# The last store as a plain DMA of the framework, with ScalarE taking the waits for the six stores ahead of it

## Chip, cores, metric

One core of one Trainium2 chip. The metric is the device time of one execution in microseconds (us), as the median of several runs. The "span" of a profile is the time from the core's first to its last instruction, some 1.8 us shorter than the device time here (123.5 against 125.36 us in the profiled run of the kernel before).

## The reference

Sixteen products of 512 x 512 matrices in float32, the second operand transposed:

```python
def setup_inputs():
    batch, m, k, n = 16, 512, 512, 512
    # a: (batch, m, k), b: (batch, n, k), standard normal float32
def reference(a, b):
    return np.matmul(a, b.transpose(0, 2, 1)).astype(np.float32)
```

## The kernel before

Loads, casts, transposes, products, evictions and stores run on their own engines and talk through semaphores that the kernel allocates itself. All of it stands in one hand-written section (`tile_critical`) inside which the framework adds no waits. When a section is left, the framework closes it: the engine that leads the section (SyncE, if nothing else is said) raises a semaphore, waits for the engines, and only then goes on. In the trace a closing shows as a branch, an event, a drain and a no-op: instructions without data, which here only wait for semaphores or count them up (records of 33, 17, 7 and 13 ns in the kernel before). A second, tiny section holds one wait, that for the last store.

```python
    STORES = "SSSSOSOSOSSOOOOOO"          # GpSimd stores outputs 0 to 7
    LATE = {11: (8, 9), 13: (10, 11), 15: (12, 13)}   # SyncE stores 8 to 15
    NO = 7                                 # output buffers
    ...
        def store(n):
            engine = nc.gpsimd if n < STORES.count("S") else nc.sync
            engine.wait_ge(s_out, n + 1)   # ScalarE counts finished outputs
            engine.dma_start(
                out[n].rearrange("(p j) n -> p j n", j=J), ob[:, n % NO]
            ).then_inc(landed(n)[0], 16)
        ... # loads, with late stores between them
        store(batch - 2)
        store(batch - 1)
        for n in range(batch - NO, batch - 1):
            nc.sync.wait_ge(*landed(n))    # stores 9 to 14 have landed
        ... # programs of GpSimd, VectorE, ScalarE, TensorE

    with tc.tile_critical(no_gpsimd_drain=True):
        nc.sync.wait_ge(*landed(batch - 1))   # store 15 has landed
```

## Time and profile before

| | before |
|---|---|
| device time, median | 125.48 us (125.31 to 125.68, 6 runs) |
| span of the profiled run | 123.5 us |
| mean rate from HBM and to it | 407 GB/s |
| ScalarE's last copy ends | 113.474 us |
| last store issued / landed | 113.499 / 122.217 us |
| SyncE joins the barrier at the end | 122.698 us |
| last instruction ends | 123.549 us |

The first three rows are from the results and the page. The others, with three decimals, are records of the trace: starts of single instructions, and the times at which a DMA adds to its semaphore. The trace has 16 such additions for each store; a store has landed when the last has come. I read each as one of the core's 16 DMA engines having done its part; the trace itself doesn't name the engine. Read the table from below: between the last landing and the end of the span lie 1.332 us in which no byte moves (the last packet of the trace ends at 121.751). The lines of the profile are shown in the prediction.

### The profile page before, as it was taken

The numbers are of one execution on the slowest core, as the hardware profiler recorded it, in microseconds if no ns is written. First come the engines' busy times: TensorE is split into PE (matmuls) and PEld (weight loads), VectorE is DVE, ScalarE is ACT, GpSimd is POOL, SyncE is SP. The second block draws the span as 40 slices with busy tenths as digits, with TensorE's granted clock in tenths as the row PEclk, the third lists the DMA queues.
The fourth block names the chain that finished last, engine by engine and source line by source line (L and its number), as shares of the span: only waits on it lengthen the run. The fifth ranks groups of instructions, "written<-read, shape, count | busy, mean of one in ns | idle before, by whom it ended". The sixth has DMA issues, their size and how long they took to land. (4 is left out here: it accounts for less than half of the span.)

```text
span 123.5 us, 2364 instructions
## 1 busy us (share of the span) xinstructions
PE 90.7 (73%) x768; PEld 55.8 (45%) x768; DVE 67.9 (55%) x96; ACT 68.1 (55%) x130; POOL 5.9 (5%) x14
## 2 busy tenths in 40 slices
PE   0000089999899999989998999899999946994000
PEld 0000079546734774476467447644764535441000
DVE  0000597891898389568928991894787078400000
ACT  4000063458946885595769558937876069555000
POOL 2000000000000160001010230000000000000000
PEclk9999999999999999999999999999999999999955
DMA  4999999999999999999999999999999999999990
GB/s 127 419 446 435 424 424 430 424 424 424 430 430 435 424 403 385 461 390 427 454 400 454 424 414 454 411 432 446 416 438 419 416 427 422 430 424 427 430 385 11
DMA packets 4608, 50.33 MB, mean 407 GB/s; under 512 B 512, under 2 KB 512, under 8 KB 512
## 3 DMA queue, kind: packets, MB, share of 16 engines
q1 hardware_dynamic: 3312, 39.85, 76.2%
q0 software_dynamic: 1152, 8.39, 16.1%
q10 hardware_dynamic: 144, 2.10, 4.3%
HBM read 33.55 MB, written 16.78 MB: 407 GB/s over the span
## 5 line engine op out<-in xcount | busy, mean ns | idle before, releaser
L255 PE MATMUL ps<-tb,ta 128*128 128x512 bf16 x256 | 57.8, 379 | 0.5
L213 ACT COPY ob<-ps 128x512 f32 x64 | 34.5, 588 | 28.5 <-PE ps L255 24.6
L195 ACT COPY ta<-tp 128x512 bf16<-128x512 bf16 x64 | 32.8, 610 | 15.4 <-PE tp L236 15.4
L255 PEld LDWEIGHTS ps<-tb,ta 128*128 128x128 bf16 x256 | 24.1, 97 | 30.7 <-issue 4.0
L236 PE MATMUL tp<-ident,ha 128*128 128x128 bf16 x256 | 19.6, 230 | 19.3 <-PEq L141 19.3
L236 PEld LDWEIGHTS tp<-ident,ha 128*128 128x128 bf16 x256 | 16.6, 103 | 23.1 <-issue 21.3
L176 DVE COPY tb<-tp 128x1024 bf16<-128x1024 bf16 x32 | 21.2, 684 | 4.8 <-DVEq L141 4.8
L236 PE MATMUL tp<-ident,hb 128*128 128x128 bf16 x256 | 18.1, 227 | 2.2 <-PEq L141 2.2
L236 PEld LDWEIGHTS tp<-ident,hb 128*128 128x128 bf16 x256 | 16.1, 102 | 2.6 <-issue 2.6
L160 DVE CAST ha<-ld 128x1024 bf16 x8 | 5.5, 686 | 13.7 <-DVEq L141 13.7
L171 DVE COPY ha<-wa 128x2048 bf16<-128x2048 bf16 x8 | 5.5, 692 | 13.6 <-DVEq L141 13.6
L166 DVE CAST wa<-ld 128x2048 bf16 x8 | 9.8, 1227 | 0.0
L166 DVE CAST wb<-ld 128x2048 bf16 x8 | 9.7, 1218 | 0.0
L160 DVE CAST hb<-ld 128x1024 bf16 x8 | 5.5, 688 | 6.4 <-DVEq L141 6.4
L109 POOL DMA_DIRECT2D out_dram<-ob x8 | 5.2, 655 | 65.2 <-DMA ld<-in_b_dram 41.1
L175 DVE COPY hb<-wb 128x2048 bf16<-128x2048 bf16 x8 | 5.5, 684 | 0.1
L163 DVE CAST ha<-ld 128x1024 bf16 x8 | 5.5, 686 | 0.0
L163 DVE CAST hb<-ld 128x1024 bf16 x8 | 5.5, 683 | 0.0
L186 ACT ACT_TABLE_LOAD x1 | 1.3, 1283 | 1.5 <-SPq L44 1.5
L80 POOL TENSOR_SCALAR_AFFINE_SELECT ident<-ident 128x128 bf16<-128x128 bf16 x1 | 0.3, 282 | 0.2 <-POOL ident L78 0.2
L78 POOL MEMSET ident<- 128x128 bf16 x1 | 0.2, 204 | 0.5 <-SPq L44 0.5
L186 ACT COPY one<-const-float32-1.0 128x1 f32<-128x1 f32 x1 | 0.2, 191 | 0.0
(4 smaller groups left out, 0.4 us busy)
## 6 DMA issues: line engine op xcount, KB each, us to landing
ld<-in_a_dram SPq DMA_DIRECT2D x8, 2048.0 KB, 26.3
ld<-in_b_dram SPq DMA_DIRECT2D x7, 2048.0 KB, 29.8
out_dram<-ob POOLq DMA_DIRECT2D x8, 1024.0 KB, 29.0
out_dram<-ob SPq DMA_DIRECT2D x8, 1024.0 KB, 19.6
ld<-in_b_dram ACTq DMA_DIRECT2D x1, 2048.0 KB, 12.2
```

The lines of the kernel that those rows point to most:

```text
L109: engine.dma_start(out[n].rearrange("(p j) n -> p j n", j=J), ob[:, n % NO]).then_inc(landed(n)[0], 16)
L160: nc.vector.tensor_copy(out=h[:, :J, :], in_=src[:, :J, :HK]).then_inc(s_cd, 1)
L163: nc.vector.tensor_copy(out=h[:, J:, :], in_=src[:, J:, :HK]).then_inc(s_c, 1)
L166: nc.vector.tensor_copy(out=w[:], in_=src[:, :, HK:]).then_inc(s_w, 1)
L171: nc.vector.tensor_copy(out=ha[:], in_=wa[:]).then_inc(s_ca, 1)
L175: nc.vector.tensor_copy(out=hb[:], in_=wb[:]).then_inc(s_cb, 1)
L176: nc.vector.tensor_copy(out=tb[:, ko, :], in_=tp[:, 2 + ko % 2].rearrange("k j p -> k (j p)"),).then_inc(s_eb, 1)
L186: nc.scalar.copy(out=one[:], in_=nc.const_aps.tensor(1.0, (P, 1), f32))
L195: c = nc.scalar.copy(out=ta[:, ko, e * J * P:(e + 1) * J * P].rearrange("k (j p h) -> k j p h", j=J, h=2), in_=tp[:, ko % 2, :, e * HP:(e ...
L213: c = nc.scalar.copy(out=dst[:, j, :].rearrange("m (p j) -> m p j", j=2 * J), in_=ps[:, j, :].rearrange("m (j p) -> m p j", j=2 * J),)
L236: t = nc.tensor.transpose(tp[:, 2 * x + g, j, :], h[:, j, g * P:(g + 1) * P], ident[:])
L255: t = nc.tensor.matmul(ps[:, j, :], ta[:, ko, (e * J + j) * P:(e * J + j + 1) * P], tb[:, ko, :].rearrange("k (j p) -> k j p", j=2 * J)[:, ...
```

## The change

Its intent is to let the end of the kernel wait for the last store without a section around that wait. The last store is no longer issued in the first section but behind all sections, as a DMA that the framework tracks. The framework's own end of the kernel waits for such DMAs anyway. The six waits for the stores ahead of it must then not hold SyncE up, since SyncE is to issue the last store. They go into the second section, which is now led by ScalarE, idle by then. The extra dependency only fixes the order in the program.

```diff
         store(batch - 2)
-        store(batch - 1)
-        for n in range(batch - NO, batch - 1):
-            nc.sync.wait_ge(*landed(n))
 ...
-    with tc.tile_critical(no_gpsimd_drain=True):
-        nc.sync.wait_ge(*landed(batch - 1))
+    with tc.tile_critical(sync_engine=act, no_gpsimd_drain=True):
+        for n in range(batch - NO, batch - 1):
+            nc.scalar.wait_ge(*landed(n))
+    waits = nc.cur_bb.bb.instructions[-1]
+    last = nc.sync.dma_start(
+        out[batch - 1].rearrange("(p j) n -> p j n", j=J), ob[:, (batch - 1) % NO]
+    )
+    tc.add_manual_dep(
+        last.ins,
+        waits.name,
+        mybir.DependencyInfo(mybir.DependencyClass.NoSync, mybir.DependencyReason.DATA),
+        reason="order of issue",
+    )
```

## The prediction

> **What bounds the kernel now.** I read the page first (rows of slices, DMA queues), then the waits of SyncE's queue, then single lines of SyncE in narrow windows at the end of the span, and last the records of the trace one by one to the nanosecond; times below with three decimals are from those records. The page says that the kernel is a stream of transfers:
>
> ```profile
> PE 90.7 (73%) x768; PEld 55.8 (45%) x768; DVE 67.9 (55%) x96; ACT 68.1 (55%) x130; POOL 5.9 (5%) x14
> ...
> DMA  4999999999999999999999999999999999999990
> GB/s 127 419 446 435 424 424 430 424 424 424 430 430 435 424 403 385 461 390 427 454 400 454 424 414 454 411 432 446 416 438 419 416 427 422 430 424 427 430 385 11
> ...
> q1 hardware_dynamic: 3312, 39.85, 76.2%
> q0 software_dynamic: 1152, 8.39, 16.1%
> q10 hardware_dynamic: 144, 2.10, 4.3%
> HBM read 33.55 MB, written 16.78 MB: 407 GB/s over the span
> ```
>
> The reader is to see that the DMA row is at 9 in 38 of 40 slices while the busiest compute engine has 73%: 50.3 MB at the some 425 GB/s of the middle slices are 118 us of the 123.5. Only the last slice is empty of transfers. So a change that moves no bytes can save only at the two ends. The chain of compute ends early:
>
> ```profile
> 112.38 0.36 ACT ob L213
> 112.74 0.06 issue
> 112.80 0.05 ACTq L213
> 112.85 0.04 issue
> 112.89 0.59 ACT ob L213
> ```
>
> ScalarE's last copy ends at 113.48, 10 us before the end; what remains is the drain of stores. SyncE's waits after 112 us:
>
> ```profile
> SPq L127 <- DMA out_dram<-ob: 5.8, 3, 2.4
> SPq L109 <- ACT ob L213: 1.8, 1, 1.8
> SPq L295 <- DMA out_dram<-ob: 1.7, 1, 1.7
> ```
>
> L109 is the issue of the last store, which waits for ScalarE; L127 are the waits for the six other late stores, and L295 that for the last store. Issue and landing of the last store, from the DMA view of 112 to 124 us, and then SyncE's own instructions in 122.2 to 122.5 and 122.5 to 122.65:
>
> ```profile
> out_dram<-ob SPq DMA_DIRECT2D x1, 1024.0 KB, 8.7
> ```
>
> ```profile
> L295 SPq EVENT_SEMAPHORE  x1: 1698/1698/1698, 120.5 to 120.5; - x1
> L295 SPq COMPARE_BRANCH  x1: 33/33/33, 122.3 to 122.3; - x1
> ```
>
> ```profile
> L268 SPq EVENT_SEMAPHORE  x1: 17/17/17, 122.4 to 122.4; - x1
> ```
>
> ```profile
> L268 SPq DRAIN  x1: 7/7/7, 122.5 to 122.5; - x1
> L268 SPq NOP  x1: 13/13/13, 122.6 to 122.6; - x1
> ```
>
> The wait of 1698 ns ends with the last store's landing. After it SyncE still runs the closing instructions of the second section (L268) before it may join the barrier at the end. That stretch is serial, with nothing beside it.
>
> [...] the L268 instructions last 7 to 17 ns, yet their starts, 122.432, 122.517 and 122.590, are 73 to 85 ns apart. So starts must be subtracted, not durations added. [...] this trace has a record of 33 ns but 155 ns from its start to the next start (122.277 to 122.432; 119.809 to 119.964 across two branches, too), and I use 155. [...] they land at 114.824, 117.290, 119.728 and 122.217, one per 2.45 us, that is 428 GB/s. [...] the 13 instruction-fetch packets in the trace all come before the first instruction.
>
> **The change, part by part.**
> 1. Removed: SyncE's waits at L127. They overlap the transfers of the last stores (the last of them ends at 119.77, the last landing is at 122.217). Worth 0.
> 2. Moved: the last store. Before, SyncE waits directly for ScalarE's copy count and starts the issue at 113.499, 16 ns after the count at 113.483. Now the first section must close first. SyncE tells the engines early (its last issue there is that at 111.320), ScalarE's drain comes after its copy, some 113.50; then SyncE passes a wait, a no-op and one branch to the issue. The old close of that section at 120 us gives the steps: wait for ScalarE to no-op 72 ns (120.201 to 120.273), no-op to next 73 (120.273 to 120.346), branch 155. Together 0.30, so the issue starts near 113.8, not 113.5. Is that on the path? The first issue of the kernel (ScalarE's, at 0.91) had its first packet at 1.937, 1.03 us later: descriptors of the last store would be ready near 114.85. The engines finish the store ahead of it between 117.6 and 119.25 (its 16 completion packets). Slack 2.8 us on the fastest engine. Worth 0; time from issue to landing should shrink from 8.7 to about 8.4 us.
> 3. Moved: the six waits, to ScalarE. The latest lands at 119.728. By the instruction order of the built program ScalarE then passes five more waits (64 ns each, as 120.415 to 120.479), a branch (155), an event (85), a drain (73), a no-op (44) and a branch (155): 0.83 us, so it is at the end barrier near 120.6, 1.6 us before the last landing. Worth 0.
> 4. Removed from behind the last landing: the section's branch, event, drain and no-op on SyncE. In the new order the wait for the framework's DMA count is followed by the drain that heads the end block. Before, branch start to start of that drain is 122.277 to 122.634, 0.357 us. After, that drain stands where the branch stood. Saved: 0.357, all on the path. By steps: branch 0.155 + event 0.085 + drain 0.073 + no-op 0.044 = 0.357.
> 5. Added: two semaphores (ScalarE's of the second section, the framework's DMA count), so the clearing of semaphores in the end clears 36, not 34. In the trace 34 clears stretch from 123.052 to 123.226, 5.3 ns each: +0.011 on the path.
> 6. Unchanged: bytes, queue and shape of the last store (128 rows of 2,048 floats on the same queue), all loops, the barrier and clear after SyncE's arrival (122.698 to 123.55).
>
> Sum: 0 + 0 + 0 - 0.357 + 0.011 = -0.35 us. 125.49 - 0.35 = 125.14, 0.28% less; the span should go from 123.5 to 123.2.
>
> **The rivals.**
> (a) The later issue is exposed: if the transfers needed the last store's descriptors earlier than I think, up to 0.30 would come back and the time would be about 125.45. For it: nothing[...]. Against: 2.8 us of slack[...]. It would take a stall over 2.8 us to lose anything.
> (b) ScalarE's closing chain replaces SyncE's: SyncE's final wait also asks for ScalarE's count of that section. If the chain were to come after the last landing the saving would vanish, and the time be 125.5 or more. The 1.6 us speak against it; its length would have to triple.
> (c) The framework's closing drain costs more after a DMA of its own than the 7 ns of the old one: then perhaps half of the saving remains, 125.3. In the trace every drain of SyncE has 7 ns, so I take this as unlikely.
> (d) An engine takes longer to the barrier: GpSimd has a drain of 714 ns at 120.084 in the old kernel. It now starts earlier, near 113.6, so it stays hidden.
> (e) Compute or transfers shift by other reasons. The streams are the same instruction by instruction up to 111 us, so only run-to-run noise, 125.47 to 125.68 in three runs, remains.
>
> **Range and chances.** The step sizes leave perhaps 0.08 us of doubt about the saving, and the three runs scatter by 0.2, with their median near the low side, so 125.14 with 0.25 below and 0.3 above: 124.90 to 125.45, which holds rival (c) and most of (a). A change of 2% is 2.5 us, seven times the whole stretch after the landing that the change touches; 2% slower would need a stall over 5 us. I put 0.01 on faster and 0.01 on slower.
>
> **What would show each step.** Part 2: SyncE's last issue starts near 113.8 and lands after about 8.4 us; the landing itself stays at 122.2. Part 3: ScalarE's last wait of the second section ends near 119.75, and ScalarE is in the end barrier before 121. Part 4: behind the last landing SyncE shows a wait and two drains, no event and no no-op, and GpSimd's barrier step comes 0.16 us after the landing, where it was 0.51 (122.730; 0.513 - 0.357). Part 5: the clear record is 223 ns before, some 234 after. I am wrong if the last landing itself moves by more than 0.1 us, if SyncE after the landing waits for ScalarE, or if the store's issue comes after 116 us.

The sum: -0.357 + 0.011 = -0.346 us, from parts 4 and 5. In the paragraph with most of the cuts, "they" are the last four stores. Part 2 and rival (a) speak of descriptors; the trace shows packets alone. That the last store could have its first packet near 114.85 was my estimate, from the 1.03 us between the kernel's first issue and its first packet.

## The result, and the profile after

The changed kernel takes 125.15 us (median of 6 runs, 124.99 to 125.43), the kernel before 125.48 us (6 runs). The ratio is 0.9976, with a 95% interval of 0.9961 to 0.9990. Ratios in this document are the mean time of one kernel's fast runs over that of the other's of the same rounds, so not quite the ratio of the medians; in the experiments the profiled run is left out of them. All runs were fast, that is, none was more than 1.5% above the fastest of its kernel. The gain of 0.33 us is there, but small.

SyncE's waits after 112 us in the changed kernel (us in total, times, longest):

```profile
SPq L109 <- ACT ob L210: 10.1, 1, 10.1
SPq L304 <- DMA out_dram<-ob: 7.0, 1, 7.0
SPq L44 <- PEq L44: 0.9, 1, 0.9
SPq L304 <- PEq L304: 0.7, 2, 0.6
SPq L44 <- ACTq L44: 0.7, 1, 0.7
```

The three waits of L127 for stores are gone. One wait of 7.0 us for a store is left, in the end block (L304, 1.7 us at L295 before). New are the two waits of L44, for TensorE and ScalarE: SyncE now stands at the close of the first section before its last issue. That issue, and then SyncE's instructions in 122.4 to 122.6 and all engines' of L304 in 122.6 to 122.7:

```profile
L270 SPq DMA_DIRECT2D out_dram<-ob x1: 332/332/332, 115.0 to 115.0; - x1
...
DMA to landing us min/median/max: 7.4/7.4/7.4
```

```profile
L304 SPq EVENT_SEMAPHORE  x1: 28/28/28, 122.5 to 122.5; - x1
L304 SPq DRAIN  x1: 7/7/7, 122.6 to 122.6; - x1
```

```profile
L304 SPq DRAIN  x1: 7/7/7, 122.6 to 122.6; - x1
L304 POOLq EVENT_SEMAPHORE  x1: 17/17/17, 122.7 to 122.7; - x1
```

Behind the last landing there are a wait and two drains, and GpSimd follows at once. The branch, event, drain and no-op of before (L295 and L268 in the prediction) have no counterpart. In the records, counted from the last landing: before, branch at 0.060, event 0.215, drain 0.300, no-op 0.373, drain 0.417, joining drain 0.481, end 1.332 us. After: wait 0.016, drain 0.089, joining drain 0.149, end 1.001 us. So 0.331 us less from the last landing to the end, and the medians differ by 0.33.

The record of 1698 ns in the prediction is a wait that shows inside its own record. In the kernels before and after, only event records that wait on two semaphores show this (713, 867 and 1698 ns, of 7 before and 8 after); none of the 290 and 291 that wait on one has a record over 51 ns. The wait for the last store has 1698 ns before, where its semaphore is the second of two, and 28 ns after, where it is the first.

The profiled run doesn't show that gain in its span: 123.5 us both times. Its last landing came at 122.474 us, 0.257 later than before. It was behind by 0.10 us already at 61 us, at an instruction that the change doesn't touch (SyncE's last load issue, at 61.091 against 60.985). How far the landing wanders without any change is the first thing that the experiments measure.

One more thing is later: the last issue, at 115.037. ScalarE's last copy ended 1.38 us later than before (114.853), because TensorE was slower just then. The stretch from 104 to 108 us, before and then after (columns: stretch, length, busy time and count of PE, PEld, DVE, ACT and POOL, then granted clock, the share of its full clock that TensorE had, DMA share, GB/s):

```profile
104.00:108.00 4.00, 3.88 (x36) 2.38 (x37) 1.85 (x3) 2.62 (x6) 0.00 (x0) 1.00 1.01 426
```

```profile
104.00:108.00 4.00, 3.69 (x29) 3.00 (x30) 2.20 (x4) 2.22 (x5) 0.00 (x0) 0.60 1.02 428
```

The granted clock was 0.60 there. The unchanged kernel, run again below, had 0.63 in the same stretch and its last issue at 114.797, so this is no effect of the change. The transfers (426 and 428 GB/s) didn't notice.

### The profile page after: what moved, and what is told of

Same layout as the page of the kernel before. It is cut to its first block, busy times and chain, and to the rows that moved or that the text cites. A ratio compares the mean times of both kernels' runs of the same rounds, so it can differ in the third digit from the quotient of the medians.

```text
span 123.5 us, 2365 instructions
## 1 busy us (share of the span) xinstructions
PE 91.8 (74%) x768; PEld 57.0 (46%) x768; DVE 68.1 (55%) x96; ACT 68.1 (55%) x130; POOL 6.2 (5%) x14
## 5 line engine op out<-in xcount | busy, mean ns | idle before, releaser
L233 PE MATMUL tp<-ident,ha 128*128 128x128 bf16 x256 | 20.1, 233 | 19.5 <-PEq L138 19.5
L233 PE MATMUL tp<-ident,hb 128*128 128x128 bf16 x256 | 18.8, 232 | 2.4 <-PEq L138 2.4
L233 PEld LDWEIGHTS tp<-ident,hb 128*128 128x128 bf16 x256 | 16.8, 105 | 2.8 <-issue 2.8
```

What stands on the lines that cost most here:

```text
L233: t = nc.tensor.transpose(tp[:, 2 * x + g, j, :], h[:, j, g * P:(g + 1) * P], ident[:])
```

## The experiments

Theory: what was gained is the closing of a section that SyncE went through behind the last landing; the landing itself doesn't move. Rivals: the plain DMA lands or is counted faster; or it is the move of the six waits, or the new time of issue, that gains. Nine more runs were made, all correct, each in five rounds and against the unchanged kernel on the same chip. They came on two chips, on which its median was 125.30 and 125.40 us. From each profile I took the last landing, and the time from it to SyncE's joining drain and to the end:

| kernel | median us | ratio to before (95%) | last landing | to joining drain | to end |
|---|---|---|---|---|---|
| before (first profile) | 125.48 | | 122.217 | 0.481 | 1.332 |
| before, again | 125.49 | 1.0012 (0.9997 to 1.0026) | 122.427 | 0.481 | 1.332 |
| changed (first profile) | 125.15 | 0.9976 (0.9961 to 0.9990) | 122.474 | 0.149 | 1.001 |
| changed, again | 125.12 | 0.9985 (0.9973 to 0.9998) | 122.149 | 0.150 | 1.002 |
| waits on SyncE behind the store | 125.56 | 1.0018 (1.0004 to 1.0031) | 122.270 | 0.519 | 1.380 |
| five sections | 128.37 | 1.0238 (1.0225 to 1.0252) | 122.373 | 3.486 | 4.337 |
| all waits in the second section | 125.75 | 1.0028 (1.0013 to 1.0043) | 122.213 | 0.824 | 1.675 |
| last store 3 us later | 125.14 | 0.9979 (0.9966 to 0.9991) | 122.321 | 0.144 | 0.997 |
| plain store, waits kept | 127.19 | 1.0143 (1.0128 to 1.0158) | 124.052 | 0.134 | 0.994 |

### Both kernels once more

No edit.

> The kernel before, unchanged, against itself: the size of what is no effect. Theory (closing steps behind the last landing) and every rival: ratio 1.000 within 0.001. From the last landing to SyncE's drain that joins the barrier 0.48 us, as in the first profile. If the ratio differs from 1 by 0.002 or more, the change's 0.24% can't be told from scatter.

> The changed kernel again, on the same chip as the others of this set. Theory: ratio 0.9973 (125.15 over 125.48), landing to barrier drain 0.15 us as in its first profile; the issue of the last store 0.2 us after ScalarE's last copy, and landing to the end 1.00 us against 1.33. If the first result came from a lucky set of runs: ratio 0.999 to 1.000.

The kernel before, against itself, gave 1.0012, a little more than the 0.001 that I had allowed. So ratios of this size can't be read to better than about 0.001, and the times alone would be thin evidence for 0.0024. The profiles are sharper. From the landing to the end both kernels repeat to 1 ns (1.332 and 1.332; 1.001 and 1.002), while the landing itself wanders by 0.21 us in the kernel before and by 0.33 in the changed one. All scatter lies ahead of the landing, all of the gain behind it. In this set the means of the two repeated kernels are 125.50 (6 runs) and 125.12 us (5 runs), a difference of 0.38. The issue came 0.186 us after ScalarE's last copy.

### The plain store with the six waits on SyncE behind it

```diff
-        store(batch - 1)
-        for n in range(batch - NO, batch - 1):
-            nc.sync.wait_ge(*landed(n))
 ...
+    nc.sync.dma_start(out[batch - 1]..., ob[:, (batch - 1) % NO])
     with tc.tile_critical(no_gpsimd_drain=True):
-        nc.sync.wait_ge(*landed(batch - 1))
+        for n in range(batch - NO, batch - 1):
+            nc.sync.wait_ge(*landed(n))
```

> The last store is the framework's plain DMA, as in the change, but the six waits stand in a section on SyncE behind it, so that this section waits for the plain DMA too and closes behind the last landing. Theory (the gain is the closing of a section, no longer behind the last landing): the gain is gone, ratio to before 1.000 (within 0.001), some 0.48 us from landing to the barrier drain. Rival 1 (the plain DMA itself lands or is counted faster): the gain stays, ratio 0.9975. Rival 2 (the gain comes from the later issue of the last store or from the six waits leaving the first section): the gain stays too, since both are as in the change.

The gain is gone: the ratio is 1.0018, and the rivals' 0.9975 is far outside the interval. It is even a little over the 1.000 of the theory; of that, the stretch from landing to end explains 0.05 us (1.380 against 1.332), and the rest is within what the kernel before shows against itself. SyncE's L268 instructions of this kernel (all of them), then its L296 instructions from 122.2 to 123:

```profile
L268 SPq NOP  x2: 13/13/13, 115.2 to 122.7; - x2
L268 SPq EVENT_SEMAPHORE  x1: 17/17/17, 122.5 to 122.5; - x1
L268 SPq DRAIN  x1: 7/7/7, 122.6 to 122.6; - x1
```

```profile
L296 SPq EVENT_SEMAPHORE  x2: 17/22/28, 122.3 to 122.9; - x2
L296 SPq DRAIN  x2: 7/7/7, 122.7 to 122.8; - x2
L296 SPq COMPARE_BRANCH  x1: 33/33/33, 122.4 to 122.4; - x1
```

The last store is a plain DMA and issued as in the change (114.776), but branch, event, drain and no-op stand behind its landing again, since the section behind it also waits for it. A plain DMA alone is worth nothing. What counts is that no section closes behind it.

### Five sections instead of one

```diff
+    for _ in range(5):
-    with tc.tile_critical(no_gpsimd_drain=True):
-        nc.sync.wait_ge(*landed(batch - 1))
+        with tc.tile_critical(no_gpsimd_drain=True):
+            nc.sync.wait_ge(*landed(batch - 1))
```

> The kernel before with the second section five times instead of once; four more closings behind the last landing, with no new transfer to wait for. Theory: by the starts in the profile before, one more closing is branch 155 + event 85 + drain 73 + no-op 73 + no-op 70 + three waits 64, 62 and 60 ns = 0.64 us, so four are +2.6 us: 128.1 us, ratio 1.021. Rival (closings overlap with something else, or cost nothing by themselves): 125.5, ratio 1.000. If closings cost what the change gained, 0.33 each: 126.8, ratio 1.011.

Measured: 128.37 us, a ratio of 1.0238; landing to end 4.337 us, so 3.005 more for four closings where I had added up 2.6. From branch to branch they take 0.646, 0.640, 1.047 and 0.660 us: three as reckoned, and one with a gap of 0.425 us between two waits (starts 124.256 and 124.681) where the others have 0.061. What made that gap is open. This is the only profile that has an instruction fetch within the span (one packet, 125.324 to 125.892 us), but it comes after the gap and its engine isn't recorded. The section's instructions in this profile:

```profile
L269 SPq NOP  x10: 13/13/18, 120.5 to 125.7; - x10
L269 SPq EVENT_SEMAPHORE  x5: 17/17/17, 122.6 to 125.6; - x5
L269 SPq DRAIN  x5: 7/7/7, 122.7 to 125.7; - x5
```

Five closings behind the last landing, one after another, of which none overlaps anything. More closings cost more time, each at least 0.64 us.

### All waits in the second section

```diff
-        for n in range(batch - NO, batch - 1):
-            nc.sync.wait_ge(*landed(n))
 ...
     with tc.tile_critical(no_gpsimd_drain=True):
-        nc.sync.wait_ge(*landed(batch - 1))
+        for n in range(batch - NO, batch):
+            nc.sync.wait_ge(*landed(n))
```

> The kernel before with the six waits moved from the first section into the second, beside the wait for the last store, all on SyncE. In the built program the wait for the last store then comes first of the section and the five instructions that wait for the others come behind it. Theory (what counts is how many of SyncE's instructions stand behind the last landing): five waits of 64 ns more, landing to end 1.33 + 0.32 = 1.65 us, ratio to before 1.0026. Rival (taking the six waits out of the first section is itself the gain): 0.9975. Rival (waits that are already met cost nothing): landing to end 1.33 us, ratio 1.000.

Measured: 1.0028, landing to end 1.675 us, 0.343 more. Taking the six waits out of the first section gains nothing. On the contrary: the framework puts the wait for the last store first, and five instructions whose waits have long been met follow it. SyncE's instructions of L294 from 122.2 to 123 us:

```profile
L294 SPq EVENT_SEMAPHORE  x5: 28/28/28, 122.3 to 122.5; - x5
L294 SPq COMPARE_BRANCH  x1: 33/33/33, 122.6 to 122.6; - x1
L294 SPq DRAIN  x1: 7/7/7, 123.0 to 123.0; - x1
```

Each shows 28 ns, but they start 59 to 68 ns apart. So a wait that was already met wasn't free here, behind the last landing.

### The last store some 3 us later

The changed kernel, with SyncE waiting for stores 9 to 13 in the first section as well (`range(batch - NO, batch - 2)`), so that it issues the last store after store 13 has landed.

> The changed kernel, but SyncE keeps five of the six waits, to the store before the second to last (landing near 117.4 us), in the first section, so that the last store is issued some 4 us later, near 117.9 us. Theory (the issue has slack, and the most on the DMA engine that lags by 1.2 us and ends last): last landing as before, 122.2 to 122.5 us, landing to end 1.00 us, ratio 0.9975. Fifteen engines would start their part near 118.9 and end near 121.5, later than the 121.0 of before, but still before the lagging one. Rival a of the prediction (a later issue comes back in the time): with an issue 4 us later, landing 1 us later or more, ratio over 1.005.

Measured: 0.9979, the gain of the change, with an issue at 117.985, 2.95 us later than in the changed kernel's profile and 4.5 us later than in that of before. The transfers from 112 to 124 us, in 40 slices of 0.3 us, and the time to landing:

```profile
DMA  9999999999999999999200789998999000000000
```

```profile
DMA to landing us min/median/max: 4.3/4.3/4.3
```

The DMA engines do run dry for some slices (20 to 22), and yet the end doesn't move. One DMA engine lags at the end: in the kernel before, fifteen of the sixteen completions of the last store came by 121.005 and the sixteenth at 122.217. Here the fifteen came by 121.821 and the last at 122.321. The pause costs the fifteen their lead and the time nothing. Rival (a) of the prediction, a later issue that comes back in the time, falls, with even more room than I had thought.

### The plain store with the waits kept

```diff
-        store(batch - 1)
         for n in range(batch - NO, batch - 1):
             nc.sync.wait_ge(*landed(n))
 ...
-    with tc.tile_critical(no_gpsimd_drain=True):
-        nc.sync.wait_ge(*landed(batch - 1))
+    nc.sync.dma_start(out[batch - 1]..., ob[:, (batch - 1) % NO])
```

> Only the plain last store of the change; all six waits stay on SyncE in the first section, and ScalarE waits for nothing. The last store is issued only after the landing of the one ahead of it, near 120.4 us. Theory: the engines run dry; issue 120.4 + 1.03 to the first packet + 8 packets of 0.31 us + 0.47 to the count = landing near 124.4 us, 2.1 later, less 0.33 at the end: 127.2 us, ratio 1.014. This is why ScalarE takes the waits. If the plain store without the move of the waits already gave the gain: 0.9975.

Measured: 127.19 us, 1.0143. The issue comes at 120.217, the landing at 124.052, a little before the 124.4 expected, since the issue came 0.18 us earlier and the first packet followed it after 0.83 us (120.217 to 121.050) and not 1.03. (At the start of the kernel before it was 1.02, from 0.913 to 1.937.) The transfers from 112 to 126 us, in slices of 0.35 us:

```profile
DMA  9999999999999999210000000399999980000000
GB/s 445 445 445 398 445 421 398 421 468 445 398 445 421 398 398 492 117 47 23 23 0 0 0 0 0 164 492 445 398 374 374 374 374 0 0 0 0 0 0 0
```

A hole of several slices, in which the last store hasn't been issued because SyncE waits for the one before. This is the part of the change that looks like bookkeeping and isn't: without ScalarE taking the waits, the plain store loses 1.8 us. The closing is as short as in the change (0.994 us to the end), with no second section at all.

This run also shows what the lag of the one DMA engine is. After the hole all sixteen completions of the last store came within 0.142 us (123.910 to 124.052), so no engine was slower at that store. In the kernel before, the sixteenth completion came 0.13 us after the fifteenth at the first load (13.121), 0.76 at 104.624 and 1.21 at the end, and over the last four stores it hardly grew (1.14 to 1.21). So the lag is a backlog that built up earlier in the kernel, and the "in all profiles" of the expectation below holds for the late stores alone. What builds the backlog up is open.

### Two attempts at a better version, both slower

The lag of the one DMA engine, 1.2 us, is more than the whole change gained. Splitting the last store of the changed kernel unevenly might give that engine less to do. How the rows of a transfer are dealt to the engines I had not measured; both expectations assume it.

```diff
-    last = nc.sync.dma_start(out[batch - 1]..., ob[:, (batch - 1) % NO])
+    for lo, hi in ((0, 120), (120, 128)):      # second attempt: 112, 7, 7 and 2 rows
+        last = nc.sync.dma_start(dst[lo:hi], ob[lo:hi, (batch - 1) % NO])
```

> An attempt at a better version: the changed kernel with its last store in two, 120 rows and 8 rows. In all profiles the last of the 16 completion counts of a store comes 1.2 us after the fifteenth: one DMA engine lags. If that engine is the one that 120 rows leave out[...], its part of the last store falls away and 8 others get one packet of 0.31 us more: landing near 121.4 us instead of 122.3, ratio to before 0.990. If it is one of the engines that get the 8 rows: landing 0.3 us later, ratio 1.000.

Measured: 125.78 us, 1.0030 (1.0017 to 1.0043). In the profile the last completion of both parts was late, at 122.062 and 122.362 us, so the lagging engine works on both. The time is worse than either of my cases. The profiled run was the fastest of the six (125.20; the others 125.64 to 125.93), so it doesn't show what the slow ones did; that stays open.

> A second attempt at a better version. In the run with 120 and 8 rows the last completion of both parts came late (122.06 and 122.36 us), so the lagging DMA engine is among those that an 8-row transfer uses. Here the last store of the changed kernel goes in 112, 7, 7 and 2 rows: if an n-row transfer uses the first n engines and the lagging one is the eighth, it gets 7 packets instead of 8, and the seven before it 9 or 10: landing 0.3 us earlier than in the changed kernel, near 122.0 us, and ratio to before 0.995. If the lagging engine is one of the first seven: one or two packets more, landing 0.3 to 0.6 us later, ratio 1.000 to 1.003. Theory on the closing: landing to end stays 1.00 to 1.05 us in both cases.

Measured: 126.09 us, 1.0058 (1.0034 to 1.0081). The last completions of the parts of 112, 7 and 7 rows came at 122.401, 122.722 and 123.026, about 0.3 us apart, those of the two rows at 121.039 and 121.051. By my reading the lagging engine gets a row of each 7-row part, and none of the two: the bad case, with one row more each time. Which of the engines lags, and why, stays open; I found no version that beats the changed kernel. From the landing to the end it took 1.105 us, a little over the 1.05 that I had allowed: the third part landed last, and the wait for the fourth stood behind it as one more instruction. The issues of few rows also had longer records on SyncE: 0.62 and 1.06 us with 7 rows and 1.12 with two (0.75 with 8 in the first attempt), against 0.33 us with the 128 rows of the changed kernel.

## Why the prediction was right

The time (125.14 against 125.15 measured), the gain and its place were right. That the times agree to 0.01 is luck, since the six runs lie between 124.99 and 125.43; the stretch behind the landing is the evidence. By the prediction's own steps:

1. Waits of L127, worth 0: right. With the waits taken out of the first section and nothing else gained, the kernel was slower (1.0028), by the instructions that then stood behind the landing.
2. The later issue, worth 0: right, and the slack larger than estimated: 4.5 us of delay against the kernel before cost nothing. The size of the delay was off. I had 0.30 us from ScalarE's last copy to the issue, measured were 0.184 and 0.186. The term at fault is the branch of 155 ns: in the trace the no-op (114.962) and the issue (115.037) start 75 ns apart, as two no-ops do in the kernel before (73), with no record of a branch between. In the built program there is one, but without a wait, while the branches of 155 ns all carry one. The absolute time, "near 113.8" and landing after 8.4 us, was wrong as well (115.037 and 7.4 us), since TensorE's granted clock fell just before (0.60 from 104 to 108 us); that is no part of the change.
3. ScalarE's closing, worth 0: right. I had 0.83 us from the landing of store 14 to the barrier, measured were 0.851 (120.013 to 120.864), and 1.61 us are left to the last landing, 1.6 predicted. That 0.83 came so close is luck in part. Its last branch (155 ns), again without a wait, left no record: the no-op and the barrier drain start 57 ns apart (120.807, 120.864). Against that, the five further waits took 77 ns each on ScalarE and not the 64 taken from SyncE, and 0.08 us had passed before them (to 120.094). Rival (b) falls with it. ScalarE's instructions of L304 from 120 to 121 us:

```profile
L304 ACTq EVENT_SEMAPHORE  x5: 38/38/38, 120.1 to 120.4; - x5
L304 ACTq COMPARE_BRANCH  x1: 38/38/38, 120.5 to 120.5; - x1
L304 ACTq DRAIN  x1: 8/8/8, 120.9 to 120.9; - x1
```

4. The closing removed, 0.357 us: right in kind, 0.332 in size (0.481 less 0.149 to the joining drain). The drain doesn't start where the branch stood, 0.060 us after the landing, but at 0.089; 4 ns come back in the next step. The drains have 7 ns as before, so rival (c) falls. GpSimd's step in the barrier came 0.18 us after the landing, 0.16 predicted. Its drain of 714 ns ran from 113.199, hidden as rival (d) has it; it is as early in the plain store with the waits behind it (112.932), where the gain is gone, so the gain isn't that either.
5. Two more semaphores to clear, 0.011 us: the clear record went from 223 to 226 ns, so it was 0.003.

The sum was -0.346 us, measured -0.331 from the last landing to the end. The span was to go to 123.2 us and stayed at 123.5 in the profiled run, since its last landing came 0.257 us later, the noise of rival (e). One of my own tests failed: I had said that I would be wrong if the landing moved by more than 0.1 us, and in the first profile it moved by 0.257. The repeats show that the test was too sharp: the unchanged kernel's landing moves by 0.21 us from one profile to another, and the changed kernel's two landings lie on both sides of the two of before. A reading was off too: the four stores before the change land 2.464 us apart on average, not 2.45, which is 426 GB/s and not 428; no step rests on it.

## What to carry to other kernels

Once the last transfer had landed, every instruction of the engine that waited for it was paid in full here: in the kernel before 44 to 85 ns from start to start and 155 for a branch that carries a wait, for records of 7 to 33 ns; so let that wait be the last thing of the program, with no section closing and no wait already met behind it, and give the waits that are met earlier to an engine that has time, so that the last issue doesn't stand behind them (here that would have cost five times the gain). For an effect of 0.3 us, compare the stretch between two events in the profile and not the total: the stretch repeated to 1 ns, the total scattered by more than the effect.
